# A two-layer decoder on one core: first weights through spare tiles, w_o matmuls ahead of the last mix, and eight small moves

## The chip, the cores and the metric

The kernel runs on one NeuronCore of a Trainium2 chip. Five engines work side by side, each through its own list of instructions in order: TensorE (PE) multiplies matrices into PSUM, VectorE (DVE), ScalarE (ACT) and GpSimd (POOL) work on rows, and SyncE (SP) mostly issues transfers between HBM and the on-chip memory. Engines wait for one another through semaphores. The metric is the device time of one execution in microseconds (us); lower is better.

## The reference

512 tokens of width 1024 pass two layers. Each layer is a mixer and an MLP, and behind each stands a layer norm of the scaled residual sum. The first mixer is latent attention (MLA, 8 heads, ranks 384 and 256, a rotary part of 64); the second is sliding-window attention (SWA, 16 query heads of 64 on 4 shared key/value heads, window 128, with learned sinks and a relative bias).

```python
def _mla(x, w_in, g_q, g_kv, w_uq, w_uk, w_uv, w_o, pos):
    h = x @ w_in
    c_q = _rmsnorm(h[..., :MLA_Q_RANK], g_q)
    c_kv = _rmsnorm(h[..., MLA_Q_RANK:MLA_Q_RANK + MLA_KV_RANK], g_kv)
    k_r = _rope(h[..., MLA_Q_RANK + MLA_KV_RANK:], pos)
...
    return o @ w_o

def _mlp(x, w_up, w_down):
    h = jax.nn.relu(x @ w_up)
    return (h * h) @ w_down

def reference(x, ...):
    alpha = (2 * DEPTH) ** 0.25
    for l in range(DEPTH):
...
        x = _layernorm(alpha * x + y, ln_mix_g[l], ln_mix_b[l])
        x = _layernorm(alpha * x + _mlp(x, mlp_w_up[l], mlp_w_down[l]), ln_mlp_g[l], ln_mlp_b[l])
    return x
```

## The kernel before

Every matrix product is made of three: each operand is split into a high part in the fast fp32r format and a low part, the rest (high x high, high x low, low x high). `split` (L78, L81) lets ACT copy the high part and DVE (or POOL, for the weights named in `ON_POOL`) subtract it for the low one. PE can't start a product before its low part stands.

Weights come as a stream of chunks of up to 128 x 1024. `queue` appends a chunk, `prep` and `weights` make chunks in that order, a few ahead of their use. `make` (L121 to L131) takes a raw tile (ring of 2), issues the load on SP (L129) and splits it into `wh` and `wl` (rings of 4). PSUM has eight banks: six "mm" banks for products and two "tr" banks for transposes.

PE's and most of SP's instructions stay in the order of the code (`pe`). The other engines are ordered by a list scheduler that runs its own estimate of the timeline, so an edit in one place can reorder them around it; `tc.high_priority()` and `pin` bind a few.

The stages, with their place in the profiled execution: x times w_kv and w_q (6 to 45 us; `p` and its row sums L802 to L807, with the latent queries `cq_h` and `cq_l`, L815 and L816, turned by transposes at L814); the MLA heads to 159; the product with w_o to 194; the first MLP to 520; the start of SWA to 548 (`begin`, keys and first queries); its heads to 649; w_so to 686; the second MLP to 1011; then the tail, the last layer norm.

`run_steps` writes the order of PE in the head loops. At each step come the scores of a head some steps ahead, then what `fill` has due (queries, keys, values, the first parts of the projection), then `turn` (transposes of the probabilities, `pt`; in SWA `pth` and `ptl`, L1192 and L1194), then `mix`, probabilities times values. An item of `fill` has a weight, a step by which it is due and a step before which it may not come. In SWA the scores stand two steps ahead (`AHEAD_B`), and `queries(m, part)` makes both heads 2m and 2m+1 in two parts of 12 matmuls; `query_parts` (L1135, L1136) then copies their high and low half into one tile per head, on ACT and DVE. The softmax of a head runs over both: score and bias and maximum on DVE (L1164), `nb` (L1168), exponentials on ACT (L1172), sink (`ri`, L1176), sums on DVE, the scaling on POOL.

`proj` multiplies the mixed heads by w_o or w_so: `part(t, kp)` is token tile t with one pair of chunks, left half of the columns, six matmuls; `finish` does the rest, left half first. The parts of t = 0 and 1 with kp below 3 are items of `fill`. The first layer's residual `x` is loaded at L1070 into tiles that overlay MLA's own, so these loads wait until the last mix has read them. The MLP is in seven-product form, whose first factors (`w_fac`, `XFactors`) are split as the projection ends. In the tail, `layer_norm` of the last token tile gives its last 192 columns to ACT and POOL (`LN_CUT_END`, L377 to L387).

## Time and profile before

| | us |
|---|---|
| runs | 1020.85, 1019.26, 1020.58; median 1020.58 |
| the profiled execution | 1022.03, its span 1020.2 |
| mean granted TensorE clock in it | 0.995 |

Rows of the timeline give start and length in us, the engine (PEld is PE's weight load, SPq an issue on SP), the line, the operation, output and inputs by the program's names, tile shapes and count, and in brackets the idle time before it with what ended it. Rows of stretches give for each engine its busy time and count, in the order PE, PEld, DVE, ACT, POOL, then the granted clock, the DMA engines' busy share and GB/s.

### The profile page before, as it was taken

The page shows a single profiled execution, that of the slowest core. Times are in us where ns is not written, and L with a number is a line of the kernel's source. Part 1 is how long each engine was busy: PE and PEld are TensorE (multiplying, and loading weights), DVE is VectorE, ACT ScalarE, POOL GpSimd, SP SyncE. Part 2 cuts the span into 40 slices and gives each one's busy share as a digit, 9 for nine tenths or more (in the row PEclk, how much of TensorE's full clock was granted, in tenths as well). Part 3 has the DMA queues.
Part 4 walks back from the last instruction along what each step waited for, and adds up shares of the span by engine and source line. Part 5 has one row for each costly group of instructions (what it writes and reads, how often), then busy time and mean ns, then how long its engine had stood idle before and what let it go on. Part 6 is the DMA issues. An engine that isn't in the chain of part 4 may idle for free. (4 is left out here: it accounts for less than half of the span.)

```text
span 1020.2 us, 15872 instructions
## 1 busy us (share of the span) xinstructions
PE 995.0 (98%) x6148; PEld 894.7 (88%) x6148; DVE 766.3 (75%) x1230; ACT 555.2 (54%) x848; POOL 229.9 (23%) x204
## 2 busy tenths in 40 slices
PE   8999999999999999999999999999999999999996
PEld 7878887898989989998889888889999999998985
DVE  4688875979869858887595578588886885798746
ACT  4446653457637636646145689445764664564620
POOL 0121100321211211220013665223032132122002
PEclk9999999999999999999999999999999999999999
DMA  6531116397986986973332223237798798798422
GB/s 211 159 99 45 52 42 231 59 247 195 198 182 186 194 182 171 252 138 109 99 103 94 66 81 114 81 86 201 169 219 179 164 222 167 167 264 150 108 99 82
DMA packets 60391, 149.55 MB, mean 147 GB/s; under 512 B 5228, under 2 KB 10141, under 8 KB 60317
## 3 DMA queue, kind: packets, MB, share of 16 engines
q0 software_dynamic: 24320, 58.73, 32.3%
q1 hardware_dynamic: 35852, 89.72, 26.3%
q8 instruction: 48, 0.79, 0.3%
q14 instruction: 27, 0.21, 0.1%
q10 hardware_dynamic: 144, 0.10, 0.0%
HBM read 146.41 MB, written 4.22 MB: 148 GB/s over the span
## 5 line engine op out<-in xcount | busy, mean ns | idle before, releaser
L97 PE MATMUL mm<-wh,fac 128*128 128x512 f32 (+1 forms) x944 | 293.0, 387 | 0.4 <-DVE fac L81 0.4
L78 ACT ACTIVATE wh<-wq 128x1024 fp32r<-128x1024 f32 x164 | 173.1, 1059 | 191.9 <-PE mm L97 123.9
L81 DVE TENSOR_TENSOR wl<-wq,wh 128x1024 fp32r<-128x1024 f32 x164 | 199.4, 1221 | 76.7 <-ACT wh L78 75.8
L97 PE MATMUL mm<-xth,wh 128*128 128x256 f32 (+1 forms) x936 | 245.8, 290 | 0.6 <-DVE a L687 0.5
L97 PE MATMUL mm<-xth,wl 128*128 128x256 f32 (+1 forms) x808 | 235.4, 291 | 0.0
L97 PEld LDWEIGHTS mm<-wh,fac 128*128 128x128 f32 x944 | 176.1, 188 | 36.6 <-DVE fac L81 1.9
L97 PE MATMUL mm<-xtl,wh 128*128 128x256 f32 (+1 forms) x680 | 199.7, 294 | 3.5 <-DVE xtl L81 3.5
L97 PE MATMUL mm<-wl,fac 128*128 128x512 f32 (+1 forms) x472 | 182.3, 386 | 0.0
L97 PEld LDWEIGHTS mm<-xth,wh 128*128 128x128 f32 x936 | 170.8, 192 | 4.0 <-issue 0.9
L97 PEld LDWEIGHTS mm<-xth,wl 128*128 128x128 f32 x808 | 155.4, 192 | 2.3
L78 ACT ACTIVATE wh<-raw 128x1024 fp32r<-128x1024 f32 (+4 forms) x89 | 87.9, 989 | 105.1 <-PE mm L97 59.2
L170 POOL DMA_DIRECT2D wq<-in_up x64 | 77.5, 1225 | 266.4 <-DVE wl L81 197.8
L97 PEld LDWEIGHTS mm<-xtl,wh 128*128 128x128 f32 x680 | 130.9, 192 | 7.1 <-DVE xtl L81 4.1
L81 DVE TENSOR_TENSOR wl<-raw,wh 128x1024 fp32r<-128x1024 f32 (+4 forms) x70 | 80.2, 1154 | 52.1 <-ACT wh L78 52.0
L97 PEld LDWEIGHTS mm<-wl,fac 128*128 128x128 f32 x472 | 88.8, 188 | 16.7
L170 POOL DMA_DIRECT2D wq<-in_down x48 | 42.0, 874 | 190.5 <-DVE wl L81 170.3
L350 POOL TENSOR_TENSOR rs<-v,half 128x1 f32<-128x1 f32 x24 | 28.6, 1190 | 201.5 <-DVE v L369 160.7
L81 POOL TENSOR_TENSOR wl<-raw,wh 128x1024 fp32r<-128x1024 f32 (+1 forms) x19 | 40.1, 2117 | 85.2 <-ACT wh L78 85.2
L97 PE MATMUL mm<-wl,oh 128*128 128x512 f32 x128 | 50.1, 391 | 0.7 <-DVE wl L81 0.7
L97 PE MATMUL mm<-wh,oh 128*128 128x512 f32 x128 | 50.7, 396 | 0.0
L97 PE MATMUL mm<-wh,ol 128*128 128x512 f32 x128 | 50.1, 391 | 0.0
L513 DVE TENSOR_TENSOR x<-mm,x 128x512 f32<-128x512 f32 (+1 forms) x49 | 32.9, 675 | 13.9 <-PE mm L97 13.6
(220 smaller groups left out, 1838.9 us busy)
## 6 DMA issues: line engine op xcount, KB each, us to landing
wq<-in_up POOLq DMA_DIRECT2D x64, 512.0 KB, 8.6
wq<-in_down POOLq DMA_DIRECT2D x48, 512.0 KB, 7.0
wq<-in_up SPq DMA_DIRECT2D x32, 512.0 KB, 5.8
raw<-in_down SPq DMA_DIRECT2D x28, 512.0 KB, 7.3
wq<-in_down SPq DMA_DIRECT2D x24, 512.0 KB, 7.1
raw<-in_up SPq DMA_DIRECT2D x16, 512.0 KB, 4.9
raw<-in_w_o SPq DMA_DIRECT2D x8, 512.0 KB, 3.3
raw<-in_w_sq SPq DMA_DIRECT2D x8, 512.0 KB, 3.4
```

Source lines behind the costliest of these rows:

```text
L78: high = nc.scalar.activation(dst_h, src, AF.Copy)
L81: low = (engine or nc.vector).tensor_sub(dst_l, src, f32(dst_h))
L97: pe(nc.tensor.matmul(dst, st, mv, start=first and i == 0, stop=last and i == len(pairs) - 1, **kw))
L170: nc.gpsimd.dma_start(half(a, jp), chunk(*more, jp), accum_op=ALU.add)
L350: nc.gpsimd.tensor_tensor(r, v, half, ALU.pow)
L513: nc.vector.tensor_add(xs[t][:, c], b, xs[t][:, c])
```

## The change

- **Start.** Two spare tiles of the tag "xt" are taken early. The third and fourth chunk of w_kv go into the first, the first two of w_q into the second, the last two of w_q into raw tiles; a chunk that was fetched so is split later by `make` without a load of its own. Loads of x and of the tables are pinned to SP's order, and the tables (ident, the gains, sinks, relative bias, constants) come behind these weights.
- **Engine.** The low halves of both w_qr chunks move from DVE to POOL.
- **Bank.** `pair_rotary` takes an mm bank instead of a tr bank.
- **`rest`.** `run_steps` gets a list that is run behind the fill and ahead of the last mixes: `proj.part(2, 0)` and `(2, 1)`, 12 matmuls, in both layers.
- **`begin`.** The transposes of the last token tile come inside the last chunk of the first half, behind four of its eight k steps.
- **MLP factors.** The split of step 3 is pinned in order on ACT and DVE.
- **SWA.** The due step of the queries is one later.
- **Tail.** The cut for ACT and POOL goes: DVE does all columns of the last tile, in two halves with one transfer each, on SP.

```diff
@@ -34,8 +34,6 @@
 POOL_O, POOL_SO = (0, 2), (0, 1, 2)
 WARM = 10
-LN_CUT_END = 832
-
@@ -104,6 +102,8 @@
         stream, off_ring = [], []
+        fetchers, at_hand, fetched = {}, {}, set()
+
         def tiles_of_weights(aside=None):
             if aside:
@@ -118,18 +118,27 @@
         def queue(name, ap, low=nc.vector):
+            index = len(stream)
+
             def make(pieces=1, between=None):
                 cols = ap.shape[-1]
-                raw = raw_tile()
+                raw = at_hand.pop(index) if index in at_hand else raw_tile()
                 wh, wl = tiles_of_weights()
                 for j in range(pieces):
                     c = slice(j * cols // pieces, (j + 1) * cols // pieces)
                     if between:
                         between(j)
-                    pe(nc.sync.dma_start(raw[:, c], ap[:, c]))
+                    if index not in fetched:
+                        pe(nc.sync.dma_start(raw[:, c], ap[:, c]))
                     split(wh[:, c], wl[:, c], raw[:, c], low)
                 return wh, wl
+            def fetch(raw):
+                at_hand[index] = raw
+                fetched.add(index)
+                pe(nc.sync.dma_start(raw[:, : ap.shape[-1]], ap))
+
+            fetchers[index] = fetch
             stream.append((name, make))
             off_ring.append(False)
@@ -212,8 +221,8 @@
             queue("w_q", io["w_q"][kp])
         queue("w_uv", io["w_uv"][0])
         queue("w_h", io["w_h"][0])
-        queue("w_qr", io["w_qr"][0])
-        queue("w_qr", io["w_qr"][1][:, 0:512])
+        queue("w_qr", io["w_qr"][0], nc.gpsimd)
+        queue("w_qr", io["w_qr"][1][:, 0:512], nc.gpsimd)
         for h in range(1, H):
             if h == 4:
                 queue("w_uv", io["w_uv"][1])
@@ -319,27 +328,33 @@
         def load_x(k, n):
             at = k // 4, slice(k % 4, k % 4 + n)
             src = xraw[at[0]][:, at[1], :]
-            nc.sync.dma_start(src, io["xT"][:, k : k + n, :])
+            pe(nc.sync.dma_start(src, io["xT"][:, k : k + n, :]))
             split(x0.hs[at[0]][:, at[1], :], x0.ls[at[0]][:, at[1], :], src)
         state["hold"] = len(stream)
         prep(0, 2, lambda j: load_x(j, 1))
+        spare = [xp.tile([P, 2, 1024], F32, tag="xt", bufs=8, name=nm("spare")) for _ in range(2)]
         for kp in range(1, 4):
             load_x(2 * kp, 2)
+            if kp > 1:
+                fetchers[kp](spare[0][:, kp - 2, :])
             prep(kp)
+        for i in range(4, 8):
+            fetchers[i](spare[1][:, i - 4, :] if i < 6 else raw_tile())
         state["next"] = 4
         ident = cp.tile([P, P], F32, name="ident")
-        nc.sync.dma_start(ident, io["ident"])
+        pe(nc.sync.dma_start(ident, io["ident"]))
...
         nc.gpsimd.memset(relb[32:33, :], 1.0)
-        nc.sync.dma_start(relb[0:32, :], io["rel"])
+        small = nc.sync.dma_start(relb[0:32, :], io["rel"])
+        pe(small)
@@ -368,23 +383,13 @@
             v = sp.tile([P, 1], F32, tag="v", bufs=8, name=nm("v"))
             pin(nc.vector.tensor_scalar(v, mv[:, 1:2], LN_EPS, None, ALU.add))
             r = rsqrt_of(v)
-            end = dst is None and t == NT - 1
-            cut = LN_CUT_END if end else D
-            a, b = slice(0, cut), slice(cut, D)
-            if end:
-                shift = sp.tile([P, 1], F32, tag="v", bufs=8, name=nm("v"))
-                nc.vector.tensor_scalar(shift, mv[:, 0:1], r, -1.0, ALU.mult, ALU.mult)
-                nc.scalar.activation(x[:, b], x[:, b], AF.Identity, bias=shift, scale=r)
-                nc.gpsimd.tensor_mul(x[:, b], x[:, b], gb[:, 0, b])
-                nc.gpsimd.tensor_add(x[:, b], x[:, b], gb[:, 1, b])
-            pin(nc.vector.scalar_tensor_tensor(x[:, a], x[:, a], mv[:, 0:1], gb[:, 0, a], ALU.subtract, ALU.mult))
-            pieces = [slice(0, cut // 2), slice(cut // 2, cut)] if end else [a]
-            for c in pieces:
+            pin(nc.vector.scalar_tensor_tensor(x, x, mv[:, 0:1], gb[:, 0, :], ALU.subtract, ALU.mult))
+            n = 2 if dst is None and t == NT - 1 else 1
+            for i in range(n):
+                c = slice(i * D // n, (i + 1) * D // n)
                 pin(nc.vector.scalar_tensor_tensor(x[:, c], x[:, c], r, gb[:, 1, c], ALU.mult, ALU.add))
                 if dst is None:
                     nc.sync.dma_start(out[t * P : (t + 1) * P, c], x[:, c])
-            if end:
-                nc.scalar.dma_start(out[t * P : (t + 1) * P, b], x[:, b])
         def turn_tokens(t, dst):
@@ -472,7 +477,8 @@
                     for t in range(NT):
                         self.evac(t, slice(512, D), bs[t])
-        def run_steps(units, ahead, scores, turn, mix, fill, per, lag):
+        def run_steps(units, ahead, scores, turn, mix, fill, per, lag, rest):
+
             total = sum(f[0] for f in fill)
@@ -492,6 +498,8 @@
                     mix(units[u - lag][0])
             for f in fill[at:]:
                 f[3]()
+            for f in rest:
+                f()
             for u in range(n, n + lag):
                 if (u - lag) % per == per - 1:
                     mix(units[u - lag][0])
@@ -534,11 +542,16 @@
                 cols = slice(half_ * 256, half_ * 256 + 256)
                 for i, (_, evac) in enumerate(chunks):
                     b = bank(256)
-                    feat_major(src, ws[i], b, cols)
+                    early = half_ == 0 and i == len(chunks) - 1
+                    feat_major(src, ws[i], b, cols, range(4))
+                    if early:
+                        with tc.high_priority():
+                            src.turn(NT - 1)
+                    feat_major(src, ws[i], b, cols, range(4, KD))
                     evac(cols, b)
-                    if half_ == 0 and i > 0:
+                    if half_ == 0 and i == 1:
                         with tc.high_priority():
-                            src.turn(i + 1)
+                            src.turn(NT - 2)
         class Factors:
@@ -604,7 +617,10 @@
                     state["hold"] = len(stream)
                     quarters = [f32(self.xf[i][:, n]) for i in range(2) for n in range(2)]
                     for n in (3, 6, 7, 4):
-                        split(self.part(n, 0), self.part(n, 1), self.sum(n, *quarters))
+                        a = self.sum(n, *quarters)
+                        pinned[0] = n == 3
+                        split(self.part(n, 0), self.part(n, 1), a, keep=n == 3)
+                        pinned[0] = False
         def mlp(src, gb, dst, mp):
@@ -780,7 +796,8 @@
         band = dr.tile([SQH, P, 256], F32, name="band")
         with tc.tile_pool(name="mla", bufs=1) as mp:
             const = mp.tile([P, C_ALL], F32, name="const")
-            nc.sync.dma_start(const, io["const"])
+            with tc.issue_after(small.ins):
+                nc.sync.dma_start(const, io["const"])
             cmask = const[:, C_MASK : C_MASK + 512]
             cos = const[:, C_COS : C_COS + 256].rearrange("p (t d) -> p t d", t=NT)
             sin = const[:, C_SIN : C_SIN + 256].rearrange("p (t d) -> p t d", t=NT)
@@ -853,7 +870,8 @@
             def bias_bands():
                 ohot, es = qrot[:, 0, :], qrot[:, 1, :]
-                nc.sync.dma_start(ohot[:33, :BANDW], io["oh"])
+                with tc.issue_after(small.ins):
+                    nc.sync.dma_start(ohot[:33, :BANDW], io["oh"])
                 eb = bank()
                 nc.tensor.matmul(eb[:SQH, :BANDW], relb, ohot[:33, :BANDW], start=True, stop=True)
                 nc.scalar.activation(es[:SQH, :BANDW], eb[:SQH, :BANDW], AF.Copy)
@@ -945,7 +963,7 @@
             def pair_rotary(hp):
-                pt = tbank()
+                pt = bank()
                 for t in range(NT):
                     pe(nc.tensor.transpose(pt[:, t * P : (t + 1) * P], qrot[:, t, hp * P : (hp + 1) * P], ident))
                 for j, (own, other) in enumerate(((lo, hi), (hi, lo))):
@@ -1061,7 +1079,8 @@
             pair_rotary(0)
             head_keys(1)
             head_queries(1)
-            run_steps([(h, i) for h in range(H) for i in range(NT)], AHEAD_S, scores, turn, mix, fill, NT, 2)
+            run_steps([(h, i) for h in range(H) for i in range(NT)], AHEAD_S, scores, turn, mix, fill, NT, 2,
+                      [lambda kp=kp: proj.part(2, kp) for kp in range(2)])
         xtok = top.enter_context(tc.tile_pool(name="xtok", bufs=1))
@@ -1227,7 +1246,7 @@
             fill = []
             for m in range(1, 8):
                 for part in range(2):
-                    fill.append((2.6, 2 * m - AHEAD_B - 3 + part, -9, lambda m=m, part=part: queries(m, part)))
+                    fill.append((2.6, 2 * m - AHEAD_B - 2 + part, -9, lambda m=m, part=part: queries(m, part)))
                 if m == 1:
                     for t in range(1, NT):
                         fill.append((2.6, 0, -9, lambda t=t: values(t)))
@@ -1241,7 +1260,8 @@
                 + [("w_sq", lambda cols, b: query_parts(0, cols, b))],
             )
             values(0)
-            run_steps([(h, 0) for h in range(SQH)], AHEAD_B, scores, turn, mix, fill, 1, 1)
+            run_steps([(h, 0) for h in range(SQH)], AHEAD_B, scores, turn, mix, fill, 1, 1,
+                      [lambda kp=kp: proj.part(2, kp) for kp in range(2)])
         gb = load_gb(io["ln_mix_g"][1], io["ln_mix_b"][1])
         with tc.tile_pool(name="mlp1", bufs=1) as mp:
```

The loads on SP (as `order` lists them, output tile and source): before, from ident to the third chunk of w_q.

```order
L333 DMA ident<-in_ident 128x128
L335 DMA gq<-in_g_q 128x3
L337 DMA gkv<-in_g_kv 128x2
L129 DMA raw_118<-in_w_kv 128x640
L339 DMA sink<-in_sinks 128x16
L342 DMA relb<-in_rel 32x16
L783 DMA const<-in_const 128x1024
L856 DMA qrot<-in_oh 33x384
L129 DMA raw_127<-in_w_kv 128x640
L129 DMA raw_192<-in_w_q 128x768
L129 DMA raw_222<-in_w_q 128x768
L129 DMA raw_252<-in_w_q 128x768
```

Now, from the third load of x (two k steps) to relb:

```order
L331 DMA xraw_90<-in_xT 128x1024
L139 DMA spare_106<-in_w_kv 128x640
L331 DMA xraw_90<-in_xT 128x1024
L139 DMA spare_106<-in_w_kv 128x640
L139 DMA spare_107<-in_w_q 128x768 x2
L139 DMA raw_135<-in_w_q 128x768
L139 DMA raw_137<-in_w_q 128x768
L347 DMA ident<-in_ident 128x128
L349 DMA gq<-in_g_q 128x3
L351 DMA gkv<-in_g_kv 128x2
L353 DMA sink<-in_sinks 128x16
L356 DMA relb<-in_rel 32x16
```

All of w_kv and w_q now stands ahead of every table, and four of these chunks go into the spare tiles.

ACT in the SWA loop: before, from the query copy for head 8 (q_5985) to the first exponential of head 7 (p_6038). The exponentials of head 6 (p_5961) lie between, with their sink term (ri).

```order
L1135 ACTIVATE q_5985<-mm_5902 64x512
L1172 ACTIVATE p_5961,sm_5944<-mm_5946,nb_5943 128x128
L1172 ACTIVATE p_5961,sm_5944<-mm_5946,nb_5943 128x256
L1172 ACTIVATE p_5961,sm_5944<-mm_5951,nb_5943 128x256 x2
L1176 ACTIVATE ri_5945<-nb_5943,sink 128x4
L78 ACTIVATE pth_5991<-tr_5993 128x512
L78 ACTIVATE pth_5991<-tr_6000 128x384
L1221 ACTIVATE low_6015<-mm_6006 64x512
L1135 ACTIVATE q_5986<-mm_5902 64x512
L1172 ACTIVATE p_6038,sm_6021<-mm_6023,nb_6020 128x128
```

Now, from the `low` copy ahead of head 7's exponentials (p_6016) to the query copy for head 9 (q_6041):

```order
L1240 ACTIVATE low_5993<-mm_5984 64x512
L76 ACTIVATE oh_5173<-o_5909 128x512
L1191 ACTIVATE p_6016,sm_5999<-mm_6001,nb_5998 128x128
L1191 ACTIVATE p_6016,sm_5999<-mm_6001,nb_5998 128x256
L1191 ACTIVATE p_6016,sm_5999<-mm_6006,nb_5998 128x256 x2
L1195 ACTIVATE ri_6000<-nb_5998,sink 128x4
L1154 ACTIVATE q_6040<-mm_5956 64x512
L76 ACTIVATE wh_6103<-raw_6102 128x1024
L76 ACTIVATE pth_6046<-tr_6048 128x512
L76 ACTIVATE pth_6046<-tr_6055 128x384
L1240 ACTIVATE low_6071<-mm_6062 64x512
L1154 ACTIVATE q_6041<-mm_5956 64x512
```

The copy for head 8 (now q_6040) stood ahead of the exponentials of head 6 and now stands behind those of head 7. On PE the second part of that query group ended 49 instructions ahead of the scores of head 8; now 15 are between, seven transposes and the eight matmuls of a mix.

DVE where w_so ends: before, from the first sum of the residual in the left half to the last token tile's statistics. wl_6819 and wl_6862 are the low halves of w_so's last two chunks, w_fac that of the MLP's first factor.

```order
L510 SCALAR_TENSOR_TENSOR x_1803<-x_1803,mm_6623 128x512
L507 BN_STATS bn_6830<-x_1803 128x6
L81 TENSOR_TENSOR wl_6819<-raw_6817,wh_6818 128x1024
L510 SCALAR_TENSOR_TENSOR x_1805<-x_1805,mm_6682 128x512
L510 SCALAR_TENSOR_TENSOR x_1807<-x_1807,mm_6779 128x512
L507 BN_STATS bn_6839<-x_1805 128x6
L81 TENSOR_TENSOR w_fac_6868<-wq_6866,w_fac_6868 128x1024
L507 BN_STATS bn_6848<-x_1807 128x6
L510 SCALAR_TENSOR_TENSOR x_1809<-x_1809,mm_6786 128x512
L81 TENSOR_TENSOR wl_6862<-raw_6860,wh_6861 128x1024
L507 BN_STATS bn_6857<-x_1809 128x6 x2
```

Now:

```order
L518 SCALAR_TENSOR_TENSOR x_1814<-x_1814,mm_6621 128x512
L515 BN_STATS bn_6828<-x_1814 128x6
L518 SCALAR_TENSOR_TENSOR x_1816<-x_1816,mm_6680 128x512
L515 BN_STATS bn_6837<-x_1816 128x6
L518 SCALAR_TENSOR_TENSOR x_1818<-x_1818,mm_6756 128x512
L515 BN_STATS bn_6846<-x_1818 128x6
L518 SCALAR_TENSOR_TENSOR x_1820<-x_1820,mm_6790 128x512
L79 TENSOR_TENSOR wl_6817<-raw_6815,wh_6816 128x1024
L515 BN_STATS bn_6855<-x_1820 128x6 x2
L79 TENSOR_TENSOR wl_6860<-raw_6858,wh_6859 128x1024
L79 TENSOR_TENSOR w_fac_6866<-wq_6864,w_fac_6866 128x1024
```

The low half of the last chunk (now wl_6860) went ahead of w_fac; that of the one before (wl_6817) went behind the sum of the last token tile.

More of the change, by code (lines that the diff above doesn't have):

```diff
@@ L326, in build @@
         prep(0, 2, lambda j: load_x(j, 1))
+        spare = [xp.tile([P, 2, 1024], F32, tag="xt", bufs=8, name=nm("spare")) for _ in range(2)]
         for kp in range(1, 4):
             load_x(2 * kp, 2)
+            if kp > 1:
+                fetchers[kp](spare[0][:, kp - 2, :])
             prep(kp)
+        for i in range(4, 8):
+            fetchers[i](spare[1][:, i - 4, :] if i < 6 else raw_tile())
         state["next"] = 4
         ident = cp.tile([P, P], F32, name="ident")
-        nc.sync.dma_start(ident, io["ident"])
+        pe(nc.sync.dma_start(ident, io["ident"]))
         gq = cp.tile([P, 3], F32, name="gq")
-        nc.sync.dma_start(gq, io["g_q"])
+        pe(nc.sync.dma_start(gq, io["g_q"]))
         gkv = cp.tile([P, 2], F32, name="gkv")
-        nc.sync.dma_start(gkv, io["g_kv"])
+        pe(nc.sync.dma_start(gkv, io["g_kv"]))
         sink = cp.tile([P, SQH], F32, name="sink")
-        nc.sync.dma_start(sink, io["sinks"].partition_broadcast(P))
+        pe(nc.sync.dma_start(sink, io["sinks"].partition_broadcast(P)))
         relb = cp.tile([33, SQH], F32, name="relb")
         nc.gpsimd.memset(relb[32:33, :], 1.0)
-        nc.sync.dma_start(relb[0:32, :], io["rel"])
+        small = nc.sync.dma_start(relb[0:32, :], io["rel"])
+        pe(small)
         half = cp.tile([P, 1], F32, name="half")
```

## The prediction

> **What bounds the kernel now.** I read the page's shares first, then the chain, then what TensorE (PE) waits for, then stretches of single stages, and at each wait the timeline of the engines behind it.
>
> ```profile
> PE 995.0 (98%) x6148; PEld 894.7 (88%) x6148; DVE 766.3 (75%) x1230; ACT 555.2 (54%) x848; POOL 229.9 (23%) x204
> ```
>
> PE is busy for 98% of the span, and the change adds and removes no matmul. So only what PE loses can be won: waits, stretches at half clock, and the tail after the last matmul. The waits, by who ended them:
>
> ```profile
> PE mm L97 <- DVE v L804: 1.7, 2, 1.1
> PE tr L814 <- DVE cq_l L816: 1.2, 1, 1.2
> ...
> PE tr L1020 <- DVE qr L954: 1.0, 1, 1.0
> ```
>
> Columns: who waited, for whom, us in total, times, longest. These are three of those that the change touches; each is small and belongs to one place, so the forecast is a sum of local terms. One more loss shows only in the clock: stretches with PE busy (second column after the length), and the granted clock ahead of the last two columns.
>
> ```profile
> 0.00:10.00 10.00, 7.92 (x30) 6.46 (x31) 3.09 (x5) 5.06 (x7) 1.04 (x7) 1.00 0.78 255
> 10.00:20.00 10.00, 9.72 (x67) 9.42 (x65) 6.20 (x8) 4.45 (x5) 0.00 (x0) 1.00 0.71 231
> 22.98:26.40 3.42, 1.78 (x7) 1.20 (x7) 2.68 (x9) 1.41 (x5) 0.56 (x1) 1.00 0.34 115
> 26.40:29.81 3.41, 3.35 (x10) 3.35 (x11) 3.27 (x15) 1.68 (x5) 1.10 (x2) 0.50 0.51 155
> 531.57:534.98 3.41, 1.87 (x11) 1.26 (x12) 3.29 (x7) 2.78 (x7) 0.00 (x0) 1.00 0.47 154
> 534.98:538.40 3.42, 3.42 (x18) 3.42 (x18) 2.14 (x5) 0.58 (x2) 0.00 (x0) 0.50 0.00 0
> 627.11:630.52 3.41, 2.17 (x18) 2.00 (x19) 3.31 (x10) 3.13 (x7) 1.82 (x2) 1.00 1.02 400
> ```
>
> Twice a stretch of 3.41 us at half clock (0.50) follows one in which PE was busy 52% (1.78 of 3.42) or 55% (1.87). The one at 627 with 64% was not followed by one. A half-clock stretch costs about 3.4/2 = 1.7 us. So a wait has a second price: some 1.4 to 1.6 us of idle PE inside one such stretch (3.41 less 55 to 64%) and the next runs at half speed.
>
> The Trainium skill ("TensorE: Matmul & The Clock Gate", Part 1, the section on oscillation) puts the practical limit at idle gaps above about 3.4 us. The rows differ: gaps of 0.55 and 1.15 us in one stretch were enough at 22.98, so the measurement decides. By the page's limit no wait forecast below would bring a half-clock stretch, and the sum would stand without that risk.
>
> **Start: weights through spare tiles.** The chain at w_q:
>
> ```profile
> 23.98 0.44 PE L97 MATMUL mm<-wl,xth 128*128 128x384 f32 x1 [0.55 <-DVE v L804]
> 26.46 0.69 PE L97 MATMUL mm<-wl,xth 128*128 128x384 f32 x1 [1.15 <-DVE v L804]
> 14.74 9.54 SPq L129 DMA_DIRECT2D raw<-in_w_q  x4
> 22.09 0.85 ACT L78 ACTIVATE wh<-raw 128x768 fp32r<-128x768 f32 x1 [3.49 <-DMA raw<-in_w_q]
> 22.96 0.96 DVE L81 TENSOR_TENSOR wl<-raw,wh 128x768 fp32r<-128x768 f32 x1 [3.37 <-ACT wh L78]
> ```
>
> The matmuls wait for wl. The releaser named (v, L804) only stands behind wl on DVE (wl 22.96 to 23.92). The wl waited for the load, whose issues spread over 14.74 to 24.28 because two raw tiles must come free. After the change all eight chunks are issued ahead of the tables with no ring to wait for. By 20 us 2.55 + 2.31 = 4.86 MB had moved in this trace; x (2.10), w_kv (1.31) and w_q (1.57) together are 4.98 MB, so at these rates the last w_q chunk lands near 20 us and is needed some 3 us later. The splits (four of 0.85 on ACT and 0.96 on DVE) fit into 10 to 20 us, where ACT idles 5.5 and DVE 3.8 us. Gain: 0.55 + 1.15, about 0.35 of a slow restart, and the half-clock stretch, 1.7: **3.8 us** (2.0 if the clock still drops, 4.2 at best, 0 if the loads come late).
>
> **Two banks and an engine.** DVE makes the low halves of w_qr just when cq_l is due:
>
> ```profile
> 49.26 1.23 DVE L81 TENSOR_TENSOR wl<-raw,wh 128x1024 fp32r<-128x1024 f32 x1 [1.10 <-ACT wh L78]
> 51.00 0.68 DVE L81 TENSOR_TENSOR wl<-raw,wh 128x512 fp32r<-128x512 f32 x1
> 52.20 1.40 DVE L816 SCALAR_TENSOR_TENSOR cq_l<-tr,gq,cq_h 128x512 fp32r<-128x512 f32 x2
> 55.11 0.39 PE L97 MATMUL mm<-wl,cq_h 128*128 128x512 f32 x1
> L81 POOL TENSOR_TENSOR wl<-raw,wh 128x1024 fp32r<-128x1024 f32 (+1 forms) x19 | 40.1, 2117 | 85.2 <-ACT wh L78 85.2
> ```
>
> Without those 1.91 us on DVE, cq_l can follow its high half. On POOL, idle there, the two take some 2.1 + 1.1 us; started at 49.26, as DVE's was, they end by 52.5, ahead of their first use at 55.11: **+1.0** of the 1.2 (0.9 to 1.2). pair_rotary in an mm bank: PE waits 1.0 at 79.5 since the rotary evacuation holds one of two tr banks. Six mm banks turn over there: **+1.0**, or 0 if the wait moves to an mm bank.
>
> **w_o matmuls ahead of the last MLA mix.** PE waits for pt here, 0.69 ahead of one matmul and then 0.73 from it to the next, where 0.23 is usual; that and the rows around come to some 1.4 us. The 12 matmuls put in its place take 2.8 (as the 12 from 577.22 to 579.98, below).
>
> ```profile
> 156.26 0.50 PE L97 MATMUL mm<-pt,vh 128*128 128x512 f32 x1 [0.69 <-ACT pt L78]
> 156.99 0.50 PE L97 MATMUL mm<-pt,vh 128*128 128x512 f32 x1 [0.22 <-DVE pt L81]
> ...
> 158.93 1.75 SPq L1070 DMA_DIRECT2D x<-in_x  x4
> 171.98 1.06 ACT L78 ACTIVATE wh<-raw 128x1024 fp32r<-128x1024 f32 x1 [6.48 <-DMA raw<-in_w_o]
> ```
>
> But the x loads overlay tiles that this mix still reads. They start when it ends (158.93), and the last w_o chunks stand behind them on SP and land 13 us later. The mix ends 2.8 − 1.4 = 1.4 us later, so do these loads, while PE gets to them 1.4 earlier. Their low halves are then late by about what was won: **0** (−1.0 to +1.4, the whole gap). For SWA the same edit moves no x load: 0.
>
> **SWA: queries one step later.** Now head 2m's q is finished 12 + 15 PE instructions ahead of its use rather than 49. One step of the head loop:
>
> ```profile
> 577.22 0.40 PE L97 MATMUL mm<-xth,wh 128*128 128x512 f32 x1
> 579.98 0.27 PE L1192 MATMUL tr<-ident,p 128*128 128x128 f32 x1
> 580.66 0.36 PE L97 MATMUL mm<-pth,vv 128*128 128x256 f32 x1
> 581.62 0.27 PE L97 MATMUL mm<-skh,q 128*128 128x128 f32 x1
> 582.61 0.41 PE L97 MATMUL mm<-xth,wh 128*128 128x512 f32 x1
> ...
> 584.82 0.21 DVE L1168 TENSOR_SCALAR nb<-mm,sink 128x4 f32<-128x4 f32 x1
> 586.25 0.69 DVE L1136 TENSOR_TENSOR q<-mm,q 64x512 fp32r<-64x512 f32 x1
> ...
> 585.06 0.59 ACT L1135 ACTIVATE q<-mm 64x512 fp32r<-64x512 f32 x1
> 585.67 0.37 ACT L1172 ACTIVATE p<-mm,nb 128x128 f32<-128x128 f32 x1
> 587.56 0.61 ACT L78 ACTIVATE pth<-tr 128x512 fp32r<-128x512 f32 x1
> ```
>
> On PE: queries 2.76, transposes 0.68, mix 0.96, scores 0.99. From scores of head 2m−1, those of 2m are wanted 0.99 + 2.76 + 0.68 + 0.96 = 5.4 us later. On ACT, for m = 2, 4, 5, 7, the exponentials of 2m−1 now stand ahead of q. From the start of the scores: nb after 585.03 − 581.62 = 3.4, exponentials 587.56 − 585.67 = 1.9, q 0.6, DVE's part 0.7: 6.6. PE waits 1.2 us; where oh or low (0.6 each) falls in between, 1.8. Estimate: 1.2 + 3 × 1.8 = 6.6, plus some 1.4 of the wait for ptl at 628 (below), which moves to the head before, where DVE still splits weights ahead of it: 8.0. What goes is the old loss at 628, since a query group now fills it:
>
> ```profile
> 628.16 0.30 PE L1192 MATMUL tr<-ident,p 128*128 128x128 f32 x1 [2.28 <-DVE ptl L81]
> 667.71 0.50 PE L97 MATMUL mm<-wl,oh 128*128 128x512 f32 x1 [0.75 <-DVE wl L81]
> ```
>
> 2.28, its slow restart and two small waits, 3.3 in all. Net **−4.7**. The ends: +2.5 if ACT and DVE run far enough ahead that no q is late, −9 if all seven pairs wait 1.8 (12.3 against 3.3).
>
> **The rest.** w_so: the low half of its last chunk now stands ahead of w_fac on DVE, so the 0.75 and its restart go: **+0.95** (0 to 1.0). begin(): the third transposes come while PE still has matmuls; the waits there only change name, but the gap may split over two stretches and spare the half clock: 1.7 at even odds, **+0.8**. Pinning step 3 of the MLP factors leaves the order of ACT and DVE as it was: 0.
>
> Tail:
>
> ```profile
> 1012.78 1.08 DVE L380 SCALAR_TENSOR_TENSOR x<-x,mv,gb 128x832 f32<-128x832 f32 x1
> 1014.43 1.21 DVE L383 SCALAR_TENSOR_TENSOR x<-x,rs,gb 128x416 f32<-128x416 f32 x2
> 1016.77 0.38 ACTq L387 DMA_DIRECT2D out<-x  x1
> ```
>
> The ACT and POOL piece ends the program. Without it DVE's first pass takes 1.08 × 1024/832 = 1.3, to 1014.1, still under the rsqrt; the two halves 1.21 × 512/416 = 1.5, to 1015.9. The last issue comes 0.9 us earlier, with a larger piece: **+0.9** (0.4 to 1.0).
>
> Sum: 3.8 + 1.0 + 1.0 + 0 − 4.7 + 0.95 + 0.8 + 0.9 = 3.75. The profiled run took 1022.03 (span 1020.2); less 3.75 is 1018.3. The median of the runs is 1020.58, 1.45 below the profiled one: **1016.8**.
>
> **Rivals.**
> - *No q is late* (SWA +2.5 instead of −4.7). For it: ACT idles in the steps without an output split, and the exponentials could start sooner. Against: ACT works in order, and nb comes 3.4 us after the scores. 1016.8 − 7.2 = 1009.6. Chance 0.25.
> - *The other side: waits for q drop the clock.* Decides from about 1.4 us idle in one 3.41 us stretch. Three waits of 1.8 with their three half-clock stretches, 3 × 1.7 = 5.1: 1021.9, and with all pairs late up to 1026. For it: 22.98, where 1.70 us in one stretch did it. Against: 627.11, where 2.28 split over two stretches did not. Chance 0.25.
> - *The start doesn't come*: the DMA engines are already 0.71 to 0.78 busy, the fourth x load now stands behind a w_kv chunk, and w_q lands when it did. 1016.8 + 3.8 = 1020.6. Chance 0.12.
> - *w_o chunks much later than forecast* (−1.4 more): 1018.2, inside the own range.
>
> The forecast as summed has 0.38, with 1013.5 to 1019. About 0.2%, 2 us, is what a measurement here can tell from no change. Faster: the forecast's part below 1018.5 (0.30) and the first rival: 0.54. Slower: most of the second, 0.20, and some of the third, 0.05: 0.25. Same: 0.21. Range: 1009 (first rival) to 1024 (between the second's 1021.9 and 1026).
>
> **What would show it.** Start: no wait of PE between 22 and 27 us, clock 1.00 up to 30. cq_l, qr, and wl at w_so gone from the list of waits. A wait for wl near 172 us in place of pt's. New waits "mm <- DVE q L1155" in the SWA loop: about four, 1.2 to 1.8 each; none means the first rival, and a clock of 0.50 behind them the second. The last issue some 4.5 us behind the last matmul rather than 5.3. The prediction is wrong if w_q's splits are not done when PE gets to them, or if mm banks, now also lent to pair_rotary, make scores wait.

## The result, and the profile after

The changed kernel is slower: median 1030.63 us of six runs (1026.47 to 1033.88) against 1019.41 of six runs before (1018.73 to 1020.85). The ratio is 1.0101 with a 95% interval of 1.0076 to 1.0127. The forecast was 1016.8, with a range up to 1024.

The profiled execution took 1027.33 (span 1025.4). That is 3.3 below the kernel's median, whereas the profile before, 1022.03, lies 2.6 above its own; the two profiles alone show only 5.2 of the 11.2 us. Taken at the same instructions of PE in both traces, the stages (in us, span of before less span of after, a minus is a loss):

| stage | forecast | traces |
|---|---|---|
| first products up to the first product with the latent keys | +3.8 | +3.67 |
| from there to the first MLA scores (w_qr on POOL) | +1.0 | +0.85 |
| MLA heads, last mix, w_o (bank of pair_rotary, 12 matmuls moved) | +1.0 + 0 | +1.03 |
| first MLP | 0 | −0.05 |
| begin | +0.8 | +1.61 |
| SWA heads (less the 2.73 us of the 12 moved matmuls) | −4.7 | −14.0 |
| w_so (with those 2.73) | +0.95 | +1.04 |
| second MLP | 0 | −0.39 |
| tail | +0.9 | +1.04 |

All lines but that of the SWA heads came out within 0.9 us of the forecast. The engines' busy time on the page hardly moved, but the list of PE's waits did (columns as before: us, times, longest):

```profile
PE 994.8 (97%) x6148; PEld 896.0 (87%) x6148; DVE 769.9 (75%) x1227; ACT 555.4 (54%) x847; POOL 232.7 (23%) x204
```

```profile
PE mm L95 <- DVE q L1155: 10.3, 6, 2.8
...
PE tr L401 <- DVE xtl L79: 2.0, 1, 2.0
PE tr L1211 <- DVE ptl L79: 1.9, 1, 1.9
...
PE tr L831 <- DVE cq_l L833: 0.3, 1, 0.3
```

The waits on v (really the low half of w_q) and qr are gone, cq_l's fell from 1.2 to 0.3, and a new one of 10.3 us stands on top: the SWA scores wait for q, six times. The timeline around one of them, by engine:

```profile
587.95 0.27 PE L95 MATMUL mm<-skh,q 128*128 128x128 f32 x1
593.22 0.28 PE L95 MATMUL mm<-ptl,vv 128*128 128x128 f32 x1
595.27 0.33 PE L95 MATMUL mm<-skh,q 128*128 128x128 f32 x1 [1.77 <-DVE q L1155]
...
587.62 1.16 DVE L79 TENSOR_TENSOR ptl<-tr,pth 128x512 fp32r<-128x512 f32 x2
588.70 0.29 DVE L1183 CUSTOM_DVE_ANT_0 mm<-mm,bias 128x128 f32<-128x128 f32 x1
590.64 0.69 DVE L1241 TENSOR_TENSOR o<-mm,low 64x512 f32<-64x512 f32 x1
591.36 0.22 DVE L1187 TENSOR_SCALAR nb<-mm,sink 128x4 f32<-128x4 f32 x1
...
591.36 0.63 ACT L76 ACTIVATE oh<-o 128x512 fp32r<-128x512 f32 x1 [0.88 <-DVE o L1241]
592.02 0.37 ACT L1191 ACTIVATE p<-mm,nb 128x128 f32<-128x128 f32 x1
593.72 0.30 ACT L1195 ACTIVATE ri<-nb,sink 128x4 f32<-128x4 f32 x1
593.91 0.59 ACT L1154 ACTIVATE q<-mm 64x512 fp32r<-64x512 f32 x1
...
594.53 0.68 DVE L1155 TENSOR_TENSOR q<-mm,q 64x512 fp32r<-64x512 f32 x1
```

PE has finished the query product at 591.8 and could start the scores at 593.5, which is 595.27 less the wait of 1.77. But ACT makes q only at 593.91, behind the exponentials of the head before; these began at 592.02, behind `oh`, which waited for `o` on DVE. ACT was idle for 0.88 us ahead of `oh`, with q not yet in reach because it stands later in its order. DVE's half of q ends at 595.21, and PE goes on.

The clock added to the price. These stretches of 3.41 us follow one another, PE's busy time first and the granted clock ahead of the last two columns:

```profile
566.31:569.72 3.41, 0.65 (x6) 0.50 (x6) 1.78 (x4) 3.36 (x12) 2.66 (x3) 1.00 0.45 172
569.72:573.14 3.42, 3.42 (x13) 2.94 (x13) 3.18 (x10) 0.58 (x1) 1.12 (x1) 0.50 0.01 2
593.61:597.03 3.42, 1.76 (x12) 1.63 (x13) 2.10 (x7) 3.37 (x9) 2.60 (x4) 1.00 0.09 35
597.03:600.44 3.41, 3.41 (x23) 3.00 (x22) 3.08 (x11) 1.19 (x3) 1.83 (x1) 1.00 0.01 2
631.16:634.57 3.41, 1.63 (x13) 1.35 (x11) 1.96 (x4) 3.39 (x10) 2.58 (x3) 1.00 0.00 0
634.57:637.99 3.42, 1.57 (x9) 1.54 (x8) 3.39 (x7) 1.42 (x3) 0.09 (x1) 0.50 0.34 99
637.99:641.40 3.41, 3.41 (x18) 3.41 (x17) 3.31 (x11) 1.34 (x3) 0.00 (x0) 0.50 0.89 362
```

PE worked for 19% and 48% of a stretch, and the next ran at half clock; one at half clock with 46% handed it on. After 52% at 593.61 the clock stayed, though. The differences between the six runs of this kernel fit the same cause: the mean granted clock was 0.993 in the two fastest (1026.5 and 1027.3), 0.988 to 0.990 in three (1030.4 to 1031.3), and 0.986 in the slowest (1033.9). Seven thousandths of the clock over 1030 us are about four more half-clock stretches (0.007 × 1030 / (0.5 × 3.41)), some 7 us, which is the difference of their times. That is an estimate from the clocks, since only one of the six runs has a trace.

### The profile page after: what moved, and what is told of

It is laid out like the page before. It is cut to its first block, busy times and chain, and to the rows that moved or that the text cites. A ratio compares the mean times of both kernels' runs of the same rounds, so it can differ in the third digit from the quotient of the medians.

```text
span 1025.4 us, 15857 instructions
## 1 busy us (share of the span) xinstructions
PE 994.8 (97%) x6148; PEld 896.0 (87%) x6148; DVE 769.9 (75%) x1227; ACT 555.4 (54%) x847; POOL 232.7 (23%) x204
## 5 line engine op out<-in xcount | busy, mean ns | idle before, releaser
L76 ACT ACTIVATE wh<-raw 128x1024 fp32r<-128x1024 f32 (+4 forms) x85 | 84.8, 998 | 96.1 <-PE mm L95 67.6
L79 DVE TENSOR_TENSOR wl<-raw,wh 128x1024 fp32r<-128x1024 f32 (+3 forms) x64 | 76.4, 1203 | 39.8 <-ACT wh L76 39.7
L79 POOL TENSOR_TENSOR wl<-raw,wh 128x1024 fp32r<-128x1024 f32 (+2 forms) x21 | 43.7, 2087 | 77.5 <-ACT wh L76 75.1
```

The costliest lines, as they stand in the source:

```text
L76: high = nc.scalar.activation(dst_h, src, AF.Copy)
L79: low = (engine or nc.vector).tensor_sub(dst_l, src, f32(dst_h))
```

## The experiments

Theory A: the due step of the SWA queries costs the time, by waits for q and the half-clock stretches they bring; the other edits are worth what the table says. Theory B: the edits together reorder the loop. Each kernel was timed against the kernel before on the same chip, whose median there was 1020.33 (for e1 to e4), 1019.03 (e5 to e8), 1019.8 (e9 to e11) and 1019.07 (e12). Times of different comparisons are thus alike only to about 1 us; the ratio to the kernel before is the safer figure.

**The due step alone, taken out and put in.**

```diff
# e1, from the changed kernel
-                    fill.append((2.6, 2 * m - AHEAD_B - 2 + part, -9, lambda m=m, part=part: queries(m, part)))
+                    fill.append((2.6, 2 * m - AHEAD_B - 3 + part, -9, lambda m=m, part=part: queries(m, part)))
# e2, from the kernel before: the other way round
```

> The changed kernel with the due step of the SWA queries put back (as before); all other edits stay. Theory A (the query edit alone costs the time, by waits for q and the half-clock stretches behind them): the SWA loop loses about what it lost before, 3 to 4 us, and the rest keeps its gain of about 9 us, so 1009 to 1012, with a spread of the runs under 2 us. Theory B (the loss comes from the edits together, for example the freed DVE and POOL time or the bank moved to pair_rotary reorder the loop): still above 1015.

> The kernel before with only the due step of the SWA queries one later. Theory A: waits for q of about 10 us and several half-clock stretches, 1030 to 1042, and a spread of several us. Theory B: within 3 us of before.

Without it 1014.72 (1012.63 to 1018.53, ratio 0.9947, interval 0.9931 to 0.9963). With it alone 1030.55 (1027.37 to 1031.40, ratio 1.0094, 1.0065 to 1.0124), and the same wait on top of PE's list:

```profile
PE mm L97 <- DVE q L1136: 8.4, 7, 2.8
```

So this one number costs 10 us in the kernel before and 16 in the changed one (1030.63 less 1014.72), and theory B, as stated, falls. Something of it is left, since the other edits make the same step some 6 us dearer. The two traces show more of each loss in the changed kernel (waits for q 10.3 against 8.4, for ptl 1.9 against 0.6, and three half-clock stretches in the loop against one); why was not tested. And the rest is worth 5.6 us, not the 9 of the expectation, and the spread without the due step is still 6 us. The trace of e1 holds two half-clock stretches, behind 46% busy in begin and 38% at the loop's old wait for ptl:

```profile
523.73:527.14 3.41, 1.58 (x14) 1.38 (x13) 3.41 (x5) 2.76 (x6) 0.00 (x0) 1.00 0.19 58
527.14:530.56 3.42, 3.42 (x17) 3.42 (x17) 3.05 (x6) 1.95 (x4) 0.00 (x0) 0.50 0.39 143
619.30:622.71 3.41, 1.31 (x12) 1.10 (x10) 3.31 (x12) 3.39 (x13) 0.37 (x2) 1.00 0.46 178
622.71:626.13 3.42, 3.24 (x16) 3.17 (x17) 3.29 (x9) 2.75 (x8) 1.84 (x3) 0.50 0.72 283
```

**Is it the idle time of PE that drops the clock?** Work that nobody needs, in the place of the waits:

```diff
# e3, in the scores of the changed kernel
+                    if n2 == 0 and h >= 4 and h % 2 == 0:
+                        group(b.rearrange("p a b -> p (a b)"), [(zeros[:, :P], zeros[:, P:])] * 8)
```

> The changed kernel with eight products of zeros (128x512, 8 x 0.23 = 1.8 us) put in front of the scores of heads 4, 6, 8, 10, 12 and 14, into the bank that these scores overwrite; so PE works while q is made. If the half-clock stretches are brought on by PE's idle time (theory A), these stretches go from the loop, but perhaps the one at a wait for ptl near 635, the runs lie within 2 us of one another, and the median falls to 1023 to 1027, although PE does 10.9 us of extra work. If the spread of the changed kernel has another cause (transfers, say), the spread stays and the median lies at 1030 or above.

1026.24, and four of five runs within 0.5 us (1026.02 to 1026.52; the fifth took 1028.96, at a clock of 0.993 against 0.996 to 0.998). PE does 10.9 us more, and the kernel is some 4 us faster than the changed one (ratio 1.0064, interval 1.0043 to 1.0086, against 1.0101, 1.0076 to 1.0127; the two overlap a little). The waits in its trace:

```profile
PE tr L1213 <- DVE ptl L79: 1.9, 1, 1.9
...
PE mm L95 <- DVE q L1155: 1.3, 2, 0.9
```

No stretch of the loop is at half clock in it. So the wait is the larger part of the cost, and the clock is the other part and most of the spread.

**Sooner q.** The changed kernel, but with ACT's copy of q raised by about 0.5 us in the scheduler's order:

```diff
# e9, from the changed kernel
-                    query_parts(m, slice(0, S), b)
+                    with tc.high_priority():
+                        query_parts(m, slice(0, S), b)
```

> The changed kernel with a higher priority in the scheduler for the copies that make q from the product. On ACT the copy for an even head moves from behind all exponentials of the head before to ahead of the last one and the sink term, about 0.6 us sooner. If PE's waits in the SWA loop are the time until this copy (theory A), each falls by about 0.6 us, 2.5 to 3.5 us in all, and fewer half-clock stretches follow: 1023 to 1028. If q is late because its product or the bias transfer is late, nothing changes: 1029 to 1032.

1024.82 (1021.82 to 1027.71). The waits for q fell from 10.3 to 6.5 us, still six of them:

```profile
PE mm L95 <- DVE q L1156: 6.5, 6, 1.1
PE tr L1212 <- DVE ptl L79: 3.4, 1, 3.4
```

The waits for heads 8, 10 and 14 were 1.8 and are now 1.1: half a microsecond of order on ACT takes 0.6 off each. That for head 4, whose q now stands ahead of three exponentials, fell from 2.8 to 0.9. At heads 6 and 12 ACT's copy of a weight had stood ahead of q; three exponentials stand there now, and the waits went from 0.6 and 1.6 to 1.1. So ACT's order is the cause, and not the product or a transfer. The wait for ptl grew from 1.9 to 3.4.

**The start alone** (e5: the diff's pieces in `queue`, `make`, `fetch`, the loads and the tables).

> The kernel before with the start alone: spare tiles, order of the loads, tables behind. By the prediction's term: the waits at w_q and the half-clock stretch behind them go, 3.8 us, 1016 to 1017. By the changed kernel's trace some 0.5 us of it is lost again earlier, at 7 to 12 us, where the second half of the first w_kv chunk comes later: 1017. The rival (the loads come late, nothing is won): 1019.5 to 1020.5.

1017.91 (1016.12 to 1020.40, ten runs), ratio 0.9991, interval 0.9978 to 1.0004: 1.1 us, hardly told from nothing. Yet its trace, and that of the changed kernel, show what was forecast: PE busy all through 20 to 30 us at full clock, where it had been 8.28 at 0.83 (the kernel before first, then e5).

```profile
20.00:30.00 10.00, 8.28 (x38) 7.38 (x37) 6.15 (x22) 3.98 (x11) 1.66 (x3) 0.83 0.44 134
20.00:30.00 10.00, 10.00 (x60) 9.31 (x58) 7.57 (x35) 2.24 (x8) 2.21 (x4) 1.00 0.27 86
```

What is missing: the half-clock stretch at 26.4 that the profiled run before paid (PE busy 52% ahead of it) does not come in every run. e2 and e6 have the old start too: e2 has the stretch (52% busy ahead of it), while e6 waits 1.16 us at 27.2 without it, since its grid falls so that this stretch is 66% busy:

```profile
24.92:28.33 3.41, 2.25 (x12) 1.93 (x13) 2.77 (x11) 0.91 (x3) 1.09 (x2) 1.00 0.37 129
```

The runs of the kernel before span 1016 to 1022.6 over all comparisons. And some 0.4 us (e5) to 0.9 us (the changed kernel) go at 8 us, where the second half of the first w_kv chunk comes later:

```profile
7.73 0.41 PE L95 MATMUL mm<-wh,xth 128*128 128x320 f32 x1 [0.95 <-ACT wh L76]
8.50 0.41 PE L95 MATMUL mm<-wl,xth 128*128 128x320 f32 x1 [0.36 <-DVE wl L79]
```

(the changed kernel; before, only the first of these two waits was there, with 0.54).

**The w_o matmuls ahead of the last MLA mix**, alone on the kernel before, and halved in the kernel without the due step:

```diff
# e6, from the kernel before: rest= in run_steps, and
+                      [lambda kp=kp: proj.part(2, kp) for kp in range(2)])
# e7, from e1, in MLA
-                      [lambda kp=kp: proj.part(2, kp) for kp in range(2)])
+                      [lambda kp=kp: proj.part(2, kp) for kp in range(1)])
```

> The kernel before with the 12 w_o matmuls ahead of the last MLA mix alone. By the prediction: the wait for pt at 156 goes (1.4 us) and a wait for the last w_o chunks of about the same size stands at 170: within 1 us of before. The rival (these chunks come in time): 1018.5 to 1019, and no new wait.

> The first kernel of the study (due step put back) with one part, 6 matmuls, ahead of the last MLA mix rather than two. If the w_o chunks are late because the mix, and with it the loads of x, ends later, the loss near 168 (2.3 us in that kernel) falls by about the 1.4 us by which the mix now ends earlier, to about 1.0, and the place as a whole wins 0.5 to 1.4 us. If the chunks are late for a reason of their own (their ring), the loss stays near 2.3.

e6 is slower than before: 1022.78 (1019.93 to 1024.69, ten runs), ratio 1.0036, interval 1.0023 to 1.0049. The wait for pt is gone; in its place, in the profile of e6:

```profile
159.13 2.34 SPq L1073 DMA_DIRECT2D x<-in_x  x4
...
172.49 1.06 ACT L78 ACTIVATE wh<-raw 128x1024 fp32r<-128x1024 f32 x1 [9.50 <-DMA raw<-in_w_o]
...
173.60 0.50 PE L97 MATMUL mm<-wh,oh 128*128 128x512 f32 x1 [0.83 <-ACT wh L78]
174.86 0.60 PE L97 MATMUL mm<-wl,oh 128*128 128x512 f32 x1 [0.76 <-DVE wl L81]
...
171.69:175.10 3.41, 1.82 (x7) 0.99 (x6) 1.48 (x2) 2.13 (x3) 0.00 (x0) 1.00 0.97 378
175.10:178.51 3.41, 3.41 (x9) 2.64 (x9) 2.20 (x2) 2.11 (x3) 0.79 (x1) 0.50 0.70 223
```

The chunks land 13.4 us after the first load of x, as they did before (13.05), with the DMA engines busy 97%. PE loses 3.7 us there, the half-clock stretch among them, against some 1.4 won; this is the trace of the slowest of the ten runs. In e7 the matmuls' loss at this place fell from 2.34 to 1.28, as it should if the mix's end sets the loads, but the time did not show it: 1014.44 (1012.57 to 1015.08), next to 1014.72.

**Other ways to fill the loop's old wait for ptl.**

```diff
# e4, from e1: w_so parts of token tile 0 due at step 11
-                    fill.append((1.3, 99, (11, 14)[t] + kp, lambda t=t, kp=kp: proj.part(t, kp)))
+                    fill.append((1.3, 11 if t == 0 and kp < 2 else 99, 11 if t == 0 and kp < 2 else (11, 14)[t] + kp, lambda t=t, kp=kp: proj.part(t, kp)))
# e8, from e1, without MLA's part of rest; in begin and in SWA's turn
+                        group(bank(), [(zeros[:, :P], zeros[:, P:])] * 8)
+                if h == 12:
+                    group(bank(), [(zeros[:, :P], zeros[:, P:])] * 8)
# e10, from e8
-                if h == 12:
+                if h == 11:
# e11, from e8 without the products in turn
-POOL_O, POOL_SO = (0, 2), (0, 1, 2)
+POOL_O, POOL_SO = (0, 2), (0, 1, 2, 3)
```

> As the first kernel, and 12 matmuls of w_so (token tile 0, first two pairs of chunks) are due at step 11 of the SWA loop rather than 13 and 14, so that they stand where PE waited 2.28 us for ptl at 628 in the kernel before. If that wait is only the time of ACT and DVE for one head, which any work on PE may cover, it goes: 2 us below the first kernel. If the wait moves on to the next step, which then has no work beside it, no difference of more than 1 us.

> The first kernel of the study, without the w_o matmuls ahead of the last MLA mix, and with eight products of zeros (1.8 us) at each of the two waits that half-clock stretches follow in its trace: ahead of the transposes of the last token tile in begin (wait of 1.8) and ahead of the transposes of head 12 (2.3). The waits are then filled with work, no stretch at half clock is left, and the runs lie within 2 us of one another, at 1010 to 1013, against 1012.6 to 1018.5 with a median of 1014.7. If the clock drops for another reason than idle PE, the spread stays near 6 us.

> As the kernel with products of zeros at two waits, but in the SWA loop ahead of the transposes of head 11, where the trace has the wait of 2.3 us, instead of head 12. Theory (idle PE brings the half-clock stretch): the wait at 620 is covered, no stretch at half clock in the loop or in begin, 1012 to 1013, runs within 1.5 us.

> As the kernel before this one, without products of zeros in the SWA loop, and with the low half of w_so's fourth chunk on POOL instead of DVE. In the traces this split (1.23 us) stands on DVE ahead of head 13's scores and of ptl, for which PE waits 2.3 us. If it causes the wait, the wait falls by about 1.2 us and stays under what brings a half-clock stretch: 1011 to 1013. If POOL then delays the scaled probabilities, the wait stays or a wait for POOL takes its place: 1014 or more.

e4: 1017.45 (1013.38 to 1019.07), so not the 2 us gain of the expectation, and probably worse than e1's 1014.72 (ratio 0.9965, interval 0.9948 to 0.9982, against 0.9947, 0.9931 to 0.9963; they overlap). The wait for ptl is gone, and the next steps, now bare, wait instead, above all for a low half of the mixed heads on POOL:

```profile
636.20 0.50 PE L95 MATMUL mm<-wh,ol 128*128 128x512 f32 x1 [1.80 <-POOL ol L79]
```

e8: 1014.10 (1013.78 to 1015.21). The products in begin work: the wait there is 0.45 us, against 1.8 in e1, and no stretch there is at half clock. Those in the loop stood one head too late, and the wait, with its stretch, was still ahead of them:

```profile
620.19 0.44 PE L1213 MATMUL tr<-ident,p 128*128 128x128 f32 x1 [2.28 <-DVE ptl L79]
```

e10, one head earlier: **1012.46** (1011.85 to 1013.12), ratio 0.9929, interval 0.9914 to 0.9945. This is the fastest kernel of the study, faster than the kernel before and the changed one: it is the changed kernel without the due step and without the MLA part, and with 16 products of zeros. Its trace has no half-clock stretch on record from 6.8 us to the last matmul:

```profile
core 0: 1010.3 us, clock 0.998
```

e11: 1015.71 (1014.25 to 1017.14). Moving the weight split from DVE to POOL only changed what PE waits for, at the same length, so that split was not the cause:

```profile
622.42 0.30 PE L1211 MATMUL tr<-ident,p 128*128 128x128 f32 x1 [2.28 <-DVE nb L1187]
```

**The MLA part once more, in the quiet kernel.** e10 with the 12 w_o matmuls ahead of the last MLA mix put back:

```diff
# e12, from e10, in MLA's run_steps
+                      [lambda kp=kp: proj.part(2, kp) for kp in range(2)])
```

> As the kernel with products of zeros ahead of the transposes of head 11 and in begin (median 1012.5), with the two w_o parts, 12 matmuls, ahead of the last MLA mix put back; so this part is weighed where no other wait brings a half-clock stretch. From the traces: the wait for pt (1.46 us) goes, the loads of x start 1.3 us later, the last w_o chunks land 13.1 to 13.5 us after them as everywhere, and PE loses 2.0 to 2.3 us for them, with a half-clock stretch (1.7) behind in some of the runs. So 1013 to 1015, slower than without, and a wider spread. If the part is neutral, as forecast: 1012 to 1013.

1015.04 (1011.99 to 1018.29): 2.6 us slower in the medians, and the spread of 6 us is back. The ratios, 0.9950 (interval 0.9931 to 0.9970) against 0.9929 (0.9914 to 0.9945), overlap, so that it is slower is likely and by how much is not settled. e12 is also e1 with the 16 products of zeros and nothing else, and is no faster than e1 (1014.72, ratio 0.9947) and no steadier: on top of e1 the zeros alone won nothing that could be measured. The kernel without the MLA part and without zeros was not run, so the 2.3 us between e1 and e10 can't be shared out between the two. The profiled run of e12 is the slowest of its six, 1018.29 (span 1015.5). It has two half-clock stretches in a row behind the wait for w_o's last chunks and nowhere else:

```profile
167.45:170.87 3.42, 1.54 (x6) 0.73 (x4) 0.57 (x1) 1.43 (x2) 0.00 (x0) 1.00 0.99 387
170.87:174.28 3.41, 2.70 (x6) 2.15 (x7) 3.10 (x3) 2.80 (x3) 0.00 (x0) 0.50 0.47 147
174.28:177.69 3.41, 3.41 (x9) 2.64 (x8) 0.98 (x2) 1.06 (x1) 1.35 (x1) 0.50 0.76 210
```

## Why the prediction was wrong

**The step that failed is "SWA: queries one step later", −4.7 net.** Its mechanism was right in the main: for heads 4, 8, 10 and 14 q stands on ACT behind the exponentials, PE waits at the scores of even heads, a wait for ptl stays, and the clock falls behind the waits. Its size was not. The prediction summed 8.0 us of waits and kept the clock out of the sum. The trace has 12.2 (10.3 + 1.9), six waits for q rather than four, and about 4.2 in three half-clock stretches (half of the 3.42, 1.57 and 3.41 us that PE was busy in them): 16.4, with slow restarts some 17.8, against 3.7 in this loop before. Of the 9.8 us between 8.0 and 17.8, 4.2 are the clock, 3.7 the waits for q, 1.4 the restarts and 0.5 the wait for ptl.

The ordinary wait for q had the right size: heads 8, 10 and 14 wait 1.8 us, the upper of the two values in the sum. What the sum left out is the copies of weights that ACT also makes in this loop, 1.06 us each. For m = 3 and 6 (heads 6 and 12) q does stand ahead of the exponentials, and was excused for it, but a weight's copy stands ahead of q, and PE waits 0.6 and 1.6 us. For head 4 such a copy stands ahead of the exponentials, and the wait is 2.8. At heads 12 and 4:

```profile
618.23 1.04 ACT L76 ACTIVATE wh<-raw 128x1024 fp32r<-128x1024 f32 x1
619.29 0.59 ACT L1154 ACTIVATE q<-mm 64x512 fp32r<-64x512 f32 x1
620.66 0.33 PE L95 MATMUL mm<-skh,q 128*128 128x128 f32 x1 [1.63 <-DVE q L1155]
...
564.78 1.06 ACT L76 ACTIVATE wh<-raw 128x1024 fp32r<-128x1024 f32 x1 [2.85 <-PE mm L95]
569.34 0.33 PE L95 MATMUL mm<-skh,q 128*128 128x128 f32 x1 [2.76 <-DVE q L1155]
```

That these waits would shrink without the copies is read from the order, not tried.

Three slips of the working change little of this. Seven waits of 1.8 come to 12.6, and to 14.0 with the 1.4 for ptl, not to 12.3. The product of q ends 15 PE instructions ahead of its use; 12 + 15 counts from the product's start. And 3.41 less 55 to 64% is 1.2 to 1.5 us, not 1.4 to 1.6.

**The rival that came true was the second**, "waits for q drop the clock", priced at 1021.9 with a bound of 1026. It was given 0.25 and the first rival, that no q is late, as much. The kernel lies beyond even that bound because the term below it was already short by some 4 us of waits, and because the prediction priced one draw of the clock: the six runs hold from about the trace's number of half-clock stretches to four more.

**Start: +3.8.** Right in the trace, +3.67. In the medians the start alone is worth 1.1 (interval from a loss of 0.4 to a gain of 2.2). The half-clock stretch counted in was that of one execution; so is the 1.7 us of begin. The 1.45 us by which the profiled run lay above the median was taken off at the end, but no term was made smaller for it.

**w_qr on POOL, +1.0, and the bank of pair_rotary, +1.0.** The wait for cq_l fell by 0.9, and that for qr is gone with no new wait on an mm bank. Neither was run alone. In e3, which has the same edits up to the SWA loop, the wait for cq_l was still 1.13: ACT's copy of w_qr stands ahead of cq_h there and waited 1.50 us for its load, against 0.68 in the changed kernel. So what POOL wins here hangs on when that load lands.

**w_o ahead of the last MLA mix, 0 (−1.0 to +1.4).** The mechanism, later loads of x and of the last chunks, was right; the loss was forecast at 1.4 and is 1.7 (changed kernel) to 2.3 (e1) without the clock, and the stall now falls into one stretch and can halve the clock. Measured: −2.6 in the quiet kernel (at intervals that overlap), −3.7 in the kernel before, where part of the 3.7 stays unexplained, since the trace of its slowest run shows 2.3 net at this place.

**w_so +0.95, tail +0.9, begin +0.8.** 1.04, 1.04 and 1.61 in the traces. The tail's last two issues:

```profile
1020.75 1.41 DVE L390 SCALAR_TENSOR_TENSOR x<-x,rs,gb 128x512 f32<-128x512 f32 x2 [0.44 <-POOL rs L365]
1021.52 0.99 SPq L392 DMA_DIRECT2D out<-x  x2
```

The last issue ends 5.1 us behind the start of the last matmul (1017.42 to 1022.51), against 6.0 before.

**Idle gaps and the clock.** The Trainium skill ("TensorE: Matmul & The Clock Gate", Part 1) speaks of idle gaps above about 3.4 us, by which no wait here would touch the clock. In these traces single waits of 1.8 to 2.8 us did in several places (1.83 at 527.0 and 2.28 at 622.9 in e1, 2.76 at 569.3 in the changed kernel), as the prediction's rows had said; the prediction chose the rows and then left their consequence out of its sum.

## What to carry to other kernels

When PE is busy for 98% of the time, a wait costs its length and, if it empties about half of a 3.4 us stretch, some 1.7 us more; so for every wait above some 1.5 us add that second price with a chance, and expect the runs to spread by it. An in-order helper engine sets what slack a producer needs: before moving work nearer to its use, ask what stands ahead of its evacuation on ACT and DVE, the copies that belong to other work included. Here one step of the loop was too little. A gain read from one profiled run should be compared with the spread of the runs before it is added up.

## What the runs showed of the hardware

- The half-clock stretches lie on a grid of 3.413 us that runs through the whole execution: in each trace their starts are whole multiples apart (137 from 169.59 to 637.22 us in e4, 180 from 9.21 to 623.61 in e11). Where PE was busy for less than 48% of a stretch at full clock, the next was at half clock every time, in the 11 traces that have such a stretch; above 60%, never, in all 14. Between 48% and 60% both happened (59% ahead of one in e5, 48% in e9 and 52% in the changed kernel ahead of none). A stretch at half clock was followed by a second one at 46% busy (changed kernel) and at 79% (e12). Counted without PE's transposes the cases separate no better: 24% ahead of none in e3, 53% ahead of one in e6. What decides there stays open; PE's ends are modelled.
- Products that nobody reads can take the place of idle PE and keep the clock: with eight of them in begin and eight ahead of head 11's transposes, e10 and e12 have no half-clock stretch at either place. Moving eight of them one head earlier took 1014.10 (e8, ratio 0.9954) to 1012.46 (e10, 0.9929). On top of e1 alone they won no time (e12), and that they narrow the runs is not shown: the four runs of e10 lie within 1.3 us, but so, within 1.4, do the four of e8, whose trace has a half-clock stretch, and the six of e12 span 6.3.
- The split of the last two w_o chunks began 12.6 to 14.4 us after the first load of x was issued, in all 14 traces: 4 MB (x 2, the norm's tables 1, w_o 1) are issued together there. With w_o matmuls ahead of the last mix it was 12.9 to 14.4, without 12.6 to 13.1. Moving the start moved the landing with it; nothing else about these loads was tried.
